# A two-layer decoder trunk on one core: four instead of three seven-product pairs in the up units, own buffers for weight halves, due times by engine

## The chip, the core and the metric

The kernel runs on one core of a Trainium2 chip. TensorE multiplies matrices into eight PSUM banks, VectorE (DVE in the profile) and ScalarE (ACT) work element by element on SBUF and PSUM, GpSimd (POOL) does little here, and SyncE (SP) issues the DMAs that bring the weights from HBM. The metric is the device time of one execution in microseconds, as a median of several runs. The time before is 2168.13 us (three runs, 2167.72 to 2169.03).

## The reference

Sequence length 256, model width 2048, two layers. Each layer has two groups of heads behind one input projection, an output projection, and an MLP with 8192 hidden columns:

```python
def hybrid_layer(x, ...):
    h = rms_norm(x, attn_norm)
    proj = h @ w_in                      # queries, keys, values, gates of both groups
    o_gla = gated linear attention (8 heads, chunks of 64), per-head rms_norm, times silu(gate)
    o_sb = stick-breaking attention (8 heads, strictly causal), per-head rms_norm
    x = x + concat(o_gla, o_sb) @ w_o    # 2048 x 2048
    hm = rms_norm(x, mlp_norm)
    up = square(relu(hm @ w_up))         # 2048 x 8192
    return x + up @ w_down               # 8192 x 2048
```

All of it is float32.

## The kernel before

**Float32 out of three matmuls.** Each operand is split into a high part, rounded to the fast float32 form of TensorE, and a low part, the rest. A product is high x high, high x low and low x high: three matmuls of 128x128 stationary by 512 moving columns. For the weights this happens on the fly: ScalarE copies the raw weights to `whi` (L1182), VectorE subtracts `raw - whi` to get `wlo` (L1186).

**Two stretches per layer.** The attention stretch (input projection, both attentions) is written in program order, with its weights split in `weight_parts` (L515). The MLP stretch begins with the last quarter of the gate projection and runs through the output projection and the MLP. It is a list of units (L1064): `g`, two `o` units, then for each of four quarters q of the hidden columns two `up` units and two `down` units (n2 = 0, 1 is the half of the columns). An `up` or `down` unit has eight pairs, a pair being 256 rows by 1024 columns of the weights (1 MB, one DMA).

**Plain and seven-product pairs.** A pair is a 2x2 by 2x2 block product: two row blocks of tokens (128 each), two blocks of the contraction, two column halves. A plain pair needs eight block products (24 matmuls) and two weight halves of 128x1024, each feeding 12 matmuls. A pair in `FAST` needs seven (21 matmuls), by Strassen's scheme in Winograd's form. For that VectorE makes three sums of raw weights (`ts` 128x1024, L1238; one 128x512 in place in `raw`, L1247; `t4` 128x512, L1243), and four things are split instead of two: row 1 of the raw pair, `t4` (half as wide), `ts`, and row 0, in this order; they feed 6, 3, 6 and 6 matmuls. The left operand needs sums too: `forms` (L391) makes four small sums on VectorE, high parts on ScalarE and low parts on VectorE. It does so for two neighbouring pairs at once if both are in the `down` list (`together`, L428). The operand of the up units is made once a layer, at the start: in `turned` (L1121), for pairs 0 to 3 behind unit o n2=0, for pairs 4 to 7 in the first two halves of the first up unit. A pair that isn't in `FAST["up"]` gets its low part by two instructions at L464. The operand of the down units is made out of each up unit's results, in `up_tail` (L1396): results are completed on VectorE (`sums_of`, `finals`), go through ReLU on ScalarE, are transposed on TensorE during the first pair of the next unit (L1427), squared, and split by `forms`.

**The planner.** The MLP stretch is scheduled by hand: each step is added to a `Plan` (L40) as a piece with an engine, an expected length, what it depends on, and a function that issues it. `run` (L68) first sets due times: TensorE's pieces are due one behind the other, without a gap; each other piece is due before the earliest of its users, less its length. Then it plays the engines forward in time: TensorE and SyncE take their pieces in list order, VectorE and ScalarE the ready piece that is due first. The order that comes out is the order of issue on each engine, and on the chip the engines follow it with semaphores.

**The ring of weight halves.** A split (`parts`, L1170) writes a pair of buffers, `whi` and `wlo`. There are five such pairs (`RING`, L1055): every fifth split uses `whi5`/`wlo5` of the pool of the MLP stretch, the others take the next one of four rotating buffers that the attention stretch uses too (`ppool`, tags `whi` and `wlo`). A split waits until TensorE has done the matmuls on the half five places before (`whi[i - RING]`, L1190). Since the four buffers rotate, splits are also tied to list order, by `last["h"]` and `last["l"]`. Raw weights have four buffers (`RAWS`), `ts` and `t4` one each.

Of the kernel before, what the change touches and what calls it, by code (L numbers as in the profile page):

```python
# [11 lines left out]
F32R = mybir.dt.float32r  # L12
# [5 lines left out]
P = 128  # L18
# [21 lines left out]
class Plan:  # L40
# [27 lines left out]
    def run(self):  # L68
        t = 0.0
        for p in self.pieces:  # L70
            if p.engine == "PE":
                p.due = t
                t += p.length
        for p in reversed(self.pieces):
            if p.engine != "PE":
                p.due = min([u.due for u in p.users], default=t) - p.length - p.lag - self.GAP
        line = {e: [p for p in self.pieces if p.engine == e] for e in ("PE", "SP")}
        free = dict.fromkeys(("PE", "SP", "DVE", "ACT"), 0.0)
        left = {p: len(p.deps) for p in self.pieces}
        at = dict.fromkeys(self.pieces, 0.0)  # L80
        ready = {"DVE": [], "ACT": []}
        order, events, count = [], [], 0
        for p in self.pieces:
            if not p.deps:
                events.append((0.0, count, p))
                count += 1
        came = set()
        while events:
            now, _, p = heapq.heappop(events)
            if p is not None:  # L90
                if p.engine in ready:
                    heapq.heappush(ready[p.engine], (p.due, count, p))
                else:
                    came.add(p)
                count += 1
            for e in free:
                if free[e] > now + 1e-9:
                    continue
                if e in ready:
                    if not ready[e]:  # L100
                        continue
                    p = heapq.heappop(ready[e])[2]
                elif line[e] and line[e][0] in came:
                    p = line[e].pop(0)
                else:
                    continue
                order.append(p)
                free[e] = now + p.length
                heapq.heappush(events, (free[e], count, None))
                count += 1  # L110
                for u in p.users:
                    at[u] = max(
                        at[u], free[e] + p.lag + (0.0 if u.engine == e else self.GAP)
                    )
                    left[u] -= 1
# [11 lines left out]
def trunk_kernel(  # L127
# [22 lines left out]
    def nm(s):  # L150
        uid[0] += 1
        return f"{s}_{uid[0]}"
# [4 lines left out]
    ppool = ctx.enter_context(tc.tile_pool(name="parts", bufs=4))  # L157
# [36 lines left out]
        return [bank_tile(b, "acc"), bank_tile(b + 1, "acc")]  # L194

    ATT = ("wg", "reset", "gmask", "mask16", "v4", "lr", "lrT", "ha", "hh", "hl", "hA", "on", "dec", "S", "kdz", "row", "bc")
    MLP = ("whi5", "wlo5", "sxh1", "sx1", "sx2", "ts", "t4", "raw2")
    MANUAL = {mybir.EngineType.PE, mybir.EngineType.DVE, mybir.EngineType.Activation}

    def tmp(tag, shape, dt=F32, bufs=2):  # L200
        pool = pools["att"] if tag in ATT else pools["mlp"] if tag in MLP else tpool
        return pool.tile(list(shape), dt, tag=tag, name=nm(tag), bufs=bufs)
# [182 lines left out]
        def both(self, k):  # L385
            return self.t[k // 2][:, k % 2].rearrange("p a t -> p (a t)")

    FAST = {"up": (1, 3, 5), "down": (2, 3, 5)}
    ORDER = {"g": (0, 1, 2, 3), "up": (0, 1, 2, 3, 4, 5, 6, 7), "down": (0, 1, 2, 3, 4, 5, 6, 7)}

    def forms(op, i, t, tag):  # L391
# [112 lines left out]
    def row_of(col):  # L504
# [7 lines left out]
        nc.vector.tensor_copy(row, pb[:, :T])  # L512
        return row

    def weight_parts(w2d, r0, c0, kt, width, fine=False, halves=1, order=lambda k: None):  # L515

        full = 2048 // kt
        raw = wpool.tile([P, kt, full], F32, tag="raw", name=nm("raw"))
        src = w2d[r0 : r0 + kt * P, c0 : c0 + width].rearrange("(k p) n -> p k n", p=P)
        step = 1 if fine else kt // halves  # L520
        for s in range(0, kt, step):
            nc.sync.dma_start(raw[:, s : s + step, :width], src[:, s : s + step, :])
        for s in range(2):
            hk = kt // 2
            hi = ppool.tile([P, hk, full], F32R, tag="whi", name=nm("whi"), bufs=4)
            lo = ppool.tile([P, hk, full], F32R, tag="wlo", name=nm("wlo"), bufs=4)
            step = 1 if fine else hk
            for q in range(0, hk, step):
                r = raw[:, s * hk + q : s * hk + q + step, :width]
                h = hi[:, q : q + step, :width]  # L530
                dep = order(s * hk + q)
                with tc.issue_after(dep) if dep else nullcontext():
                    newest["hi"] = nc.scalar.activation(h, r, AF.Copy).ins  # L533
                with tc.issue_after(st["first"]) if fine else nullcontext():
                    newest["lo"] = nc.vector.tensor_tensor(  # L535
                        lo[:, q : q + step, :width], r, f32(h), ALU.subtract
                    ).ins
            yield hi, lo
# [242 lines left out]
    for l in range(DEPTH):  # L781
# [156 lines left out]
        for b in range(2):  # L938
            t = join(unit_t(hT, wl, C_GQ + b * 256))
# [11 lines left out]
        for b in range(2):  # L951
            t = join(unit_t(hT, wl, C_GK + b * 256))
# [100 lines left out]
        add = plan.add  # L1053
        MM, TR, V2, V1, A2, A1 = 0.227, 0.108, 1.15, 0.61, 1.0, 0.55
        RING, RAWS = 5, 4  # L1055
# [20 lines left out]
        banks = {}  # L1076
        free = {}
        whi, wlo, raws = [], [], []
        up, done = {}, {}
        x_done = {}  # L1080

# [88 lines left out]
        def parts(src, readers, deps, n=2):  # L1170

            box = {}
            i = len(whi)

            def part(tag):
                if i % RING < RING - 4:
                    return tmp(tag + "5", [P, 2, 512], F32R, bufs=RING - 4)
                return ppool.tile([P, 2, 512], F32R, tag=tag, name=nm(tag), bufs=4)

            def high():  # L1180
                box["h"] = part("whi")
                nc.scalar.activation(box["h"][:, :n], src(), AF.Copy)  # L1182

            def low():
                box["l"] = part("wlo")
                nc.vector.tensor_tensor(  # L1186
                    box["l"][:, :n], src(), f32(box["h"][:, :n]), ALU.subtract
                )

            h = add("ACT", A2 if n == 2 else A1, high, deps, whi[i - RING], last.get("h"))  # L1190
            lo = add("DVE", V2 if n == 2 else V1, low, h, wlo[i - RING], last.get("l"))
            last.update(h=h, l=lo)
            whi.append([lo])
            wlo.append([])
            readers.extend((h, lo))
            return box, h, lo
# [475 lines left out]
```

## Time and profile before

| | |
|---|---|
| median of three runs | 2168.13 us |
| profiled execution: time, span | 2167.72 us, 2166.0 us |
| TensorE, VectorE, ScalarE busy | 2158.9, 1811.8, 1316.9 us |
| MLP stretch, layer 0 and 1 (first to last matmul of L1275) | 295.7 to 1087, 1372.3 to 2162 us |
| an up unit: n2=0 of a later quarter, n2=1 | 41.5, 43.3 us |
| the first up unit of a layer | 43.3 us |

Times in the profile count from the first instruction of the span. The execution takes 1.7 us more than its span, and lies 0.4 us under the median. The page groups instructions by line, engine and tiles. In a timeline a row gives start, length, engine, line, operation and tiles written and read; behind it in brackets stands the idle time of the engine before it and what ended that. A matmul's length is modelled and overlaps the next one, so pace is read from starts. VectorE's and ScalarE's instructions overlap too, by about 0.09 us, so a queue's load is less than the sum of lengths; in a table by stretches overlapping time is counted once.

### The profile page before, as it was taken

To read this page: it belongs to the slowest core of one execution; us is meant where nothing else is said; L and a number is where in the kernel's file an instruction comes from. 1 tells how busy PE (TensorE), PEld (TensorE's weight loads), DVE (VectorE), ACT (ScalarE), POOL (GpSimd) and SP (SyncE) were. 2 spreads that over 40 slices of the span, in tenths; PEclk is the share of its full clock that TensorE was granted. 3 is DMA by queue.
4 is the path that set the end of the run, shared out by engine and by line. 5 is a ranking of instruction groups with operands and counts; after the bars stand their busy time and mean duration, and the time that the engine had idled before them with its cause. 6 is when DMAs were issued, how large, how long until landed. Compare 5 with 4: busy or idle time off the path is not lost.

```text
span 2166.0 us, 27107 instructions
## 1 busy us (share of the span) xinstructions
PE 2158.9 (100%) x10352; PEld 1801.9 (83%) x10352; DVE 1811.8 (84%) x2248; ACT 1316.9 (61%) x1723; POOL 42.2 (2%) x71
## 2 busy tenths in 40 slices
PE   9999999999999999999999999999999999999999
PEld 7988888888888888888888888888888888888887
DVE  5777679998989898899857775798988999899987
ACT  5555456666566566566655554666665665665674
POOL 0020000000000000000100200000000000000000
PEclk9999999999999999999999999999999999999999
DMA  6655455565556556556546544555656655565564
GB/s 229 202 156 156 156 195 175 195 213 195 187 198 213 184 193 206 199 194 194 196 139 196 174 156 156 196 175 199 208 176 213 208 199 183 197 212 187 194 202 146
DMA packets 144358, 408.97 MB, mean 189 GB/s; under 512 B 6650, under 2 KB 31810, under 8 KB 144228
## 3 DMA queue, kind: packets, MB, share of 16 engines
q1 hardware_dynamic: 144228, 407.24, 57.0%
q8 instruction: 81, 1.33, 0.3%
q14 instruction: 49, 0.40, 0.0%
HBM read 405.12 MB, written 2.10 MB: 188 GB/s over the span
## 4 chain that ended last, share of the span: by engine, by line
PE 99%; DMA 0%; DVE 0%; SPq 0%; issue 0%; POOL 0%; ACT 0%
PE acc L552 6%; PE acc L554 6%; PE acc L553 6%; PE acc L599 3%; PE acc L603 1%; PE m__548_2787 L1275 1%; PE m__2464_11960 L1275 1%; PE m__552_2800 L1275 1%; PE m__2460_11947 L1275 1%; PE m__2561_12481 L1275 0%; PE m__2496_12142 L1275 0%; PE m__649_3321 L1275 0%; PE m__584_2982 L1275 0%; PE m__2566_12505 L1275 0%; PE m__654_3345 L1275 0%; PE m__2563_12491 L1275 0%
## 5 line engine op out<-in xcount | busy, mean ns | idle before, releaser
L1182 ACT ACTIVATE whi<-raw 128x1024 fp32r<-128x1024 f32 x592 | 617.1, 1058 | 381.4 <-PE m__2968_14364 L1275 6.9
L1186 DVE TENSOR_TENSOR wlo<-raw,whi 128x1024 fp32r<-128x1024 f32 x592 | 713.3, 1221 | 89.4 <-ACT whi L1182 83.8
L535 DVE TENSOR_TENSOR wlo<-raw,whi 128x1024 fp32r<-128x1024 f32 (+2 forms) x194 | 220.4, 1140 | 131.6 <-ACT whi L533 131.3
L533 ACT ACTIVATE whi<-raw 128x1024 fp32r<-128x1024 f32 (+2 forms) x194 | 189.8, 982 | 205.0 <-PE acc L554 156.5
L552 PE MATMUL acc<-whi,act 128*128 128x512 f32 (+2 forms) x640 | 241.7, 378 | 0.4 <-ACT act L458 0.4
L554 PE MATMUL acc<-whi,act 128*128 128x512 f32 (+2 forms) x640 | 237.0, 370 | 0.0
L553 PE MATMUL acc<-wlo,act 128*128 128x512 f32 (+2 forms) x640 | 236.2, 369 | 0.1
L1186 DVE TENSOR_TENSOR wlo<-ts,whi 128x1024 fp32r<-128x1024 f32 x104 | 127.3, 1224 | 27.4 <-ACT whi L1182 27.4
L552 PEld LDWEIGHTS acc<-whi,act 128*128 128x128 f32 x640 | 120.7, 189 | 22.5 <-issue 2.7
L554 PEld LDWEIGHTS acc<-whi,act 128*128 128x128 f32 x640 | 120.4, 188 | 20.9 <-DVE act L464 0.2
L553 PEld LDWEIGHTS acc<-wlo,act 128*128 128x128 f32 x640 | 120.7, 189 | 19.2 <-DVE wlo L535 0.6
L1058 DVE TENSOR_TENSOR ts<-raw 128x1024 f32<-128x1024 f32 x104 | 127.0, 1222 | 1.5
L1182 ACT ACTIVATE whi<-t 128x512 fp32r<-128x512 f32 x104 | 65.7, 632 | 102.6 <-DVE t L1058 90.5
L1182 ACT ACTIVATE whi<-ts 128x1024 fp32r<-128x1024 f32 x104 | 109.6, 1054 | 29.1 <-PE m__593_3021 L1275 2.1
L599 PE MATMUL acc<-act,whi 128*128 128x512 f32 x256 | 91.9, 402 | 0.0
L1186 DVE TENSOR_TENSOR wlo<-t,whi 128x512 fp32r<-128x512 f32 x104 | 71.5, 688 | 10.2 <-ACT whi L1182 10.2
L1058 DVE TENSOR_TENSOR t<-raw 128x512 f32<-128x512 f32 x104 | 71.5, 688 | 0.8
L603 PE MATMUL acc<-act,wlo 128*128 128x256 f32 x256 | 71.8, 280 | 0.0
L1058 DVE TENSOR_TENSOR raw<-ts,raw 128x512 f32<-128x512 f32 x104 | 71.3, 686 | 0.2
L599 PEld LDWEIGHTS acc<-act,whi 128*128 128x128 f32 x256 | 48.1, 188 | 11.1
L1406 ACT ACTIVATE act<-act,st 128x512 f32<-128x512 f32 x64 | 44.2, 714 | 21.3 <-DVE act L1058 21.3
L603 PEld LDWEIGHTS acc<-act,wlo 128*128 128x128 f32 x256 | 48.4, 189 | 0.1
(2130 smaller groups left out, 5007.8 us busy)
## 6 DMA issues: line engine op xcount, KB each, us to landing
raw<-in_w_up_dram SPq DMA_DIRECT2D x128, 1024.0 KB, 5.0
raw<-in_w_down_dram SPq DMA_DIRECT2D x128, 1024.0 KB, 5.2
raw<-in_w_in_dram SPq DMA_DIRECT2D x84, 1024.0 KB, 5.2
raw<-in_w_o_dram SPq DMA_DIRECT2D x32, 1024.0 KB, 5.2
raw<-in_w_in_dram SPq DMA_DIRECT2D x14, 512.0 KB, 9.3
raw<-in_w_in_dram SPq DMA_DIRECT2D x8, 544.0 KB, 3.8
out_dram<-xb SPq DMA_DIRECT2D x8, 256.0 KB, 2.7
xb<-in_x_dram SPq DMA_DIRECT2D x3, 512.0 KB, 6.9
```

What stands on the lines that cost most here:

```text
L533: newest["hi"] = nc.scalar.activation(h, r, AF.Copy).ins
L535: newest["lo"] = nc.vector.tensor_tensor(lo[:, q : q + step, :width], r, f32(h), ALU.subtract).ins
L552: nc.tensor.matmul(o, xh[:, sl], whi[:, j, :width], start=first, stop=False)
L553: nc.tensor.matmul(o, xh[:, sl], wlo[:, j, :width], start=False, stop=False)
L554: st["mm"] = nc.tensor.matmul(o, xl[:, sl], whi[:, j, :width], start=False, stop=last).ins
L599: nc.tensor.matmul(acc[f], whi[:, j, sl], op.both(k), start=(k == 0), stop=False, skip_group_check=True,)
L603: nc.tensor.matmul(acc[f][:, T:], wlo[:, j, sl], xh, start=False, stop=(k == KT - 1), skip_group_check=True,)
L1058: nc.vector.tensor_tensor(dst, a, b, op)
L1182: nc.scalar.activation(box["h"][:, :n], src(), AF.Copy)
L1186: nc.vector.tensor_tensor(box["l"][:, :n], src(), f32(box["h"][:, :n]), ALU.subtract)
L1275: nc.tensor.matmul(o, lhs, rhs, start=start and k == 0, stop=end and i + 1 == len(blocks) and k == 2, skip_group_check=onto,)
L1406: nc.scalar.activation(box[h][:, tt, :], box[h][:, tt, :], AF.Relu, scale=rr[:, tt : tt + 1],)
```

## The change

`FAST["up"]` becomes (1, 2, 4, 5) for (1, 3, 5): in each of the 16 up units four pairs instead of three go by seven products. `FAST["down"]` becomes (1, 4, 5) for (2, 3, 5), three as before. Pairs 4 and 5 now share one call of `forms` in place of 2 and 3, and `NX` keeps one more buffer for the sums of the up operand.

Each slot of the ring gets a tag with one buffer: `whi4` and `wlo4` in the MLP pool for every fifth split, and `whi0` to `whi3` and `wlo0` to `wlo3` in the pool that both stretches use, with `part_tile`. The ring stays at five. The MLP stretch picks its slots by a split's number, not by order of issue, and `part_base` carries the turn over from the attention stretch. With that the ties to list order (`last["h"]`, `last["l"]`) go.

Due times of pieces off TensorE are now set by going backward through time: of the pieces whose users are all settled, the one with the latest end comes first, and on VectorE and ScalarE it is due so that it ends before the piece of its engine that was set just before it begins. So two pieces of one engine no longer claim the same time.

```diff
@@ Plan.run
+        begins = {"DVE": t, "ACT": t}
+        unset = {p: len(p.users) for p in self.pieces if p.engine != "PE"}
+        last = []
+
+        def settled(p):
+            for d in p.deps:
+                if d in unset:
+                    unset[d] -= 1
+                    if not unset[d]:
+                        push(d)
+
+        def push(p):
+            end = min([u.due for u in p.users], default=t) - p.lag - self.GAP
+            heapq.heappush(last, (-end, -at_of[p], p))
...
         for p in reversed(self.pieces):
-            if p.engine != "PE":
-                p.due = min([u.due for u in p.users], default=t) - p.length - p.lag - self.GAP
+            if p.engine == "PE":
+                settled(p)
+        while last:
+            end, _, p = heapq.heappop(last)
+            p.due = min(-end, begins.get(p.engine, t)) - p.length
+            if p.engine in begins:
+                begins[p.engine] = p.due
+            settled(p)
@@
-    FAST = {"up": (1, 3, 5), "down": (2, 3, 5)}
+    FAST = {"up": (1, 2, 4, 5), "down": (1, 4, 5)}
@@
+    part_turn = [0]
+
+    def part_tile(tag, turn, shape):
+        slot = f"{tag}{turn % 4}"
+        return ppool.tile(shape, F32R, tag=slot, name=nm(tag), bufs=1)
+
@@ weight_parts
-            hi = ppool.tile([P, hk, full], F32R, tag="whi", name=nm("whi"), bufs=4)
-            lo = ppool.tile([P, hk, full], F32R, tag="wlo", name=nm("wlo"), bufs=4)
+            hi = part_tile("whi", part_turn[0], [P, hk, full])
+            lo = part_tile("wlo", part_turn[0], [P, hk, full])
+            part_turn[0] += 1
@@ parts
                 if i % RING < RING - 4:
-                    return tmp(tag + "5", [P, 2, 512], F32R, bufs=RING - 4)
-                return ppool.tile([P, 2, 512], F32R, tag=tag, name=nm(tag), bufs=4)
+                    return tmp(f"{tag}{4 + i % RING}", [P, 2, 512], F32R, bufs=1)
+                return part_tile(tag, i % RING - (RING - 4) + part_base, [P, 2, 512])
...
-            h = add("ACT", A2 if n == 2 else A1, high, deps, whi[i - RING], last.get("h"))
-            lo = add("DVE", V2 if n == 2 else V1, low, h, wlo[i - RING], last.get("l"))
-            last.update(h=h, l=lo)
+            h = add("ACT", A2 if n == 2 else A1, high, deps, whi[i - RING])
+            lo = add("DVE", V2 if n == 2 else V1, low, h, wlo[i - RING])
```

More of the change, by code (lines that the diff above doesn't have):

```diff
@@ L73, in run @@
                 t += p.length
-        for p in reversed(self.pieces):
-            if p.engine != "PE":
-                p.due = min([u.due for u in p.users], default=t) - p.length - p.lag - self.GAP
+        begins = {"DVE": t, "ACT": t}
[10 more added lines that the diff above has]
+            heapq.heappush(last, (-end, -at_of[p], p))
+        at_of = {p: i for i, p in enumerate(self.pieces)}
+        for p in self.pieces:
+            if p in unset and not p.users:
+                push(p)
+        for p in reversed(self.pieces):
+            if p.engine == "PE":
[6 more added lines that the diff above has]
+            settled(p)
         line = {e: [p for p in self.pieces if p.engine == e] for e in ("PE", "SP")}
@@ L196, in trunk_kernel @@
     ATT = ("wg", "reset", "gmask", "mask16", "v4", "lr", "lrT", "ha", "hh", "hl", "hA", "on", "dec", "S", "kdz", "row", "bc")
-    MLP = ("whi5", "wlo5", "sxh1", "sx1", "sx2", "ts", "t4", "raw2")
+    MLP = (*(f"{t}{i}" for t in ("whi", "wlo") for i in range(4, 12)), "sxh1", "sx1", "sx2", "ts", "t4", "raw2")
     MANUAL = {mybir.EngineType.PE, mybir.EngineType.DVE, mybir.EngineType.Activation}
@@ L1078, in trunk_kernel @@
         whi, wlo, raws = [], [], []
+        part_base = part_turn[0] % 4
         up, done = {}, {}
```

## The prediction

> **What bounds the kernel now.** I read the page first (engines, then the chain that ended last), then busy time by stretch, then the timelines of TensorE and VectorE in the two-matmul-per-weight part of the layer.
>
> ```profile
> span 2166.0 us, 27107 instructions
> ...
> PE 2158.9 (100%) x10352; PEld 1801.9 (83%) x10352; DVE 1811.8 (84%) x2248; ACT 1316.9 (61%) x1723; POOL 42.2 (2%) x71
> ...
> PE 99%; DMA 0%; DVE 0%; SPq 0%; issue 0%; POOL 0%; ACT 0%
> ```
>
> TensorE is the chain. But a busy matmul row can hide a wait, so its pace must be read from starts. Here is the first matmul of the fourth product of a seven-product pair, and the first one of the pair after it:
>
> ```profile
> 458.00 0.39 PE L1275 MATMUL m__841_4203<-whi,act 128*128 128x512 f32 x1
> ...
> 460.71 0.39 PE L1275 MATMUL m__816_4102<-whi,act 128*128 128x512 f32 x1
> ```
>
> Twelve matmuls start in 460.71 - 458.00 = 2.71 us, 0.226 us each: back to back, no wait. A product (three matmuls) is 0.68 us. So time falls one for one with matmuls removed, as long as the weight halves keep arriving. Who delivers them, and with how much room? One round of units (down n2=1, up n2=0, up n2=1, down n2=0), then the first up unit of a layer:
>
> ```profile
> core 0: us, PE busy (x) PEld busy (x) DVE busy (x) ACT busy (x) POOL busy (x), PEclk, DMA share, GB/s
> 535.29:576.77 41.48, 41.48 (x185) 34.35 (x183) 36.75 (x40) 22.11 (x24) 0.00 (x0) 1.00 0.60 198
> 576.77:618.25 41.48, 41.48 (x185) 34.35 (x183) 36.44 (x39) 23.50 (x26) 0.00 (x0) 1.00 0.61 202
> 618.25:661.55 43.30, 43.30 (x200) 36.01 (x199) 40.09 (x47) 30.39 (x38) 0.00 (x0) 1.00 0.60 200
> 661.55:704.83 43.28, 43.28 (x200) 36.00 (x199) 39.90 (x48) 30.45 (x41) 0.00 (x0) 1.00 0.59 194
> sum 169.54, PE 169.54 PEld 140.70 DVE 153.18 ACT 106.45 POOL 0.00; mean PE 42.38 PEld 35.17 DVE 38.29 ACT 26.61 POOL 0.00
> ...
> 405.42:448.71 43.29, 43.29 (x200) 36.00 (x199) 40.87 (x56) 28.41 (x42) 0.00 (x0) 1.00 0.57 194
> ```
>
> VectorE is the next bound: 153.18 of 169.54 us, so 16.4 us free in a round, and only 2.4 us in the first up unit. ScalarE has 63 us free and the DMA engines 40%. Part of VectorE's free time is not lack of work: it is ahead, and the ring of five weight halves is full. Two rows of an up unit show that:
>
> ```profile
> 601.18 1.23 DVE L1186 TENSOR_TENSOR wlo<-raw,whi 128x1024 fp32r<-128x1024 f32 x1 [1.44 <-ACT whi L1182]
> ...
> 602.81 1.06 ACT L1182 ACTIVATE whi<-raw 128x1024 fp32r<-128x1024 f32 x1 [1.66 <-PE m__1056_5204 L1275]
> ```
>
> VectorE waits for ScalarE, and ScalarE for TensorE to release a slot.
>
> **The change, part by part.** *Removed:* in each of 16 up units one pair more goes by seven products instead of eight: 16 x 3 x 0.226 = 10.9 us of TensorE. The down units keep three such pairs at other places (1, 4, 5 for 2, 3, 5): nothing on TensorE.
>
> *Added,* by these groups (the last column but one has the mean ns of one):
>
> ```profile
> L1182 ACT ACTIVATE whi<-raw 128x1024 fp32r<-128x1024 f32 x592 | 617.1, 1058 | 381.4 <-PE m__2968_14364 L1275 6.9
> L1186 DVE TENSOR_TENSOR wlo<-raw,whi 128x1024 fp32r<-128x1024 f32 x592 | 713.3, 1221 | 89.4 <-ACT whi L1182 83.8
> ...
> L1182 ACT ACTIVATE whi<-t 128x512 fp32r<-128x512 f32 x104 | 65.7, 632 | 102.6 <-DVE t L1058 90.5
> ```
>
> A plain pair costs VectorE two wide subtractions. A seven-product pair costs three wide and one narrow, and three sums (ts wide, raw and t narrow): two wide and three narrow more. What one costs the queue is the spacing of starts, not the duration:
>
> ```profile
> 637.50 1.22 DVE L1186 TENSOR_TENSOR wlo<-raw,whi 128x1024 fp32r<-128x1024 f32 x1
> 638.64 0.69 DVE L1058 TENSOR_TENSOR raw<-ts,raw 128x512 f32<-128x512 f32 x1
> 639.24 1.22 DVE L1186 TENSOR_TENSOR wlo<-raw,whi 128x1024 fp32r<-128x1024 f32 x1
> ```
>
> 1.14 us wide, 0.60 us narrow: 2 x 1.14 + 3 x 0.60 = 4.1 us more a pair, 66 us in all. ScalarE gets one wide and one narrow copy more, under 1.7 us, in 63 us of free time: no cost.
>
> The Trainium skill says otherwise about the spacing: "VectorE: DVE Perf Modes", section "The DRAIN you can't avoid", has the next operation start only when the pipeline is empty. By that a pair would cost 4.5 us, some 2 us would come on top at each tight place below, and the forecast would be about 2166. The trace does not agree (1.14 us between starts of 1.22 us operations), and the same page grants an earlier start to an operation that is not held; the sum goes by the starts.
>
> *VectorE after.* Two up units in a round: 153.2 + 8.2 = 161.4 us against 169.5 - 1.4 = 168.2 us. On the whole it fits, 96% full. Whether it fits in time is decided at the last wide subtraction of pair 5: from pair 1 on four of five pairs are now short ones, and TensorE eats such a pair in 21 x 0.226 = 4.75 us where VectorE needs 3 x 1.14 + 0.60 + 2.34 = 6.4 us.
>
> *An up unit with n2=0.* Here VectorE is through with the last unit's results and splits the narrow sum of pair 1:
>
> ```profile
> 577.92 0.69 DVE L1186 TENSOR_TENSOR wlo<-t,whi 128x512 fp32r<-128x512 f32 x1 [0.18 <-ACT whi L1182]
> ...
> 606.01 0.39 PE L1275 MATMUL m__1067_5245<-whi,act 128*128 128x512 f32 x1
> ```
>
> The last half of pair 5 was wanted at 606.01, and will be at 605.3. From 577.9 that leaves 27.4 us. Work: rest of pair 1 (0.6 + 1.14 + 1.14), pairs 2, 4, 5 (19.2), pair 3 (2.3): 24.4 us. About 3 us to spare, less some tenths of waits for ScalarE, so no stall.
>
> *An up unit with n2=1* has 1.8 us of transposes on TensorE more (43.30 against 41.48) and the forms of the down operand on VectorE. These are wanted a unit later, and due times can put them off; with pair 4 and 5 the wide form moves into the down unit, where pairs 2 and 3 leave room. No stall.
>
> *The first up unit of a layer* has no such work to put off: the forms of its own operand are wanted by its own pairs.
>
> ```profile
> 406.58 0.69 DVE L1186 TENSOR_TENSOR wlo<-t,whi 128x512 fp32r<-128x512 f32 x1 [0.18 <-ACT whi L1182]
> 412.68 0.29 DVE L405 TENSOR_TENSOR e<-t 128x128 f32<-128x128 f32 x1
> 413.94 0.87 DVE L464 SCALAR_TENSOR_TENSOR act<-m__752_3789,gcol_b,act 128x256 fp32r<-128x256 f32 x2
> 418.38 0.55 DVE L424 TENSOR_TENSOR sxh<-e,sxh 128x384 fp32r<-128x384 f32 x1
> 419.45 1.22 DVE L1186 TENSOR_TENSOR wlo<-raw,whi 128x1024 fp32r<-128x1024 f32 x1
> ...
> 436.48 0.39 PE L1275 MATMUL m__765_3844<-whi,act 128*128 128x512 f32 x1
> ```
>
> The first row is the narrow split of pair 1, the last one the use of the last half of pair 5, which comes 0.7 us earlier after. From 406.6 to 435.8 there are 29.2 us, and the work is the 24.4 us from above, forms of pairs 4 and 5 (each 1.26 for the four sums, 412.68 to 413.94, and 1.07 for the two subtractions, 418.38 to 419.45: 4.7 us together), of pairs 6 and 7 (1.6, twice 413.94 to 414.73), and up to 0.8 of norm steps that may go later: 30.7 to 31.5 us. It is late by 1.5 to 2.3 us; I take 2 us, in both layers: 4 us. TensorE takes its work in list order, so all of it stands behind that half. Bounds for each: 0, if the new order finds all of it elsewhere, and 4, if ScalarE's queue adds as much again.
>
> *Order and buffers.* Own buffers and due times add no instruction. Splits out of list order only lose two waits. The price of a bad order is unseen: from below 0; from above about 0.5 us in each of the other 14 up units, the size of the short waits for ScalarE (0.18 to 0.5 us) in front of VectorE rows. I take 0. Loads keep their number and size on SP's queue, and share 0.60 leaves them time.
>
> **Sum.** Profiled execution 2167.72 us (span 2166.0 and 1.7 around it) - 10.9 + 4.0 = 2160.8; the median of the runs is 0.4 higher, so **2161.2 us**.
>
> **Rivals.** *No stall at all:* the planner moves the forms into the gaps. For it: 3 us of room in plain units. Against: 2.4 us free in the first up unit. 2168.1 - 10.9 = 2157.2. Nothing can go lower, since TensorE has no wait left to lose.
>
> *Small stalls in every up unit:* 14 x 0.5 = 7 and 4 in the first ones: 2168.1. For it: four short pairs of five with a ring of five halves; against: down units with pairs 2 and 3 side by side run without a stall.
>
> *Slower: VectorE becomes the bound,* because its free time comes where the ring is full and can't be filled. Up units then grow by what does not fit. If half of the free time counts: n2=1 (3.2 free) 4.1 + 0.7 - 1.6 = 3.2 us, eight times; n2=0 (5.0 free) 2.3 us, six times; the first ones (2.4 free, 1.6 forms more) 5.2 us, twice: 50 us against 10.9, some 2207. At all of the free time it is 8 x 1.6 + 2 x 4.0 = 21 us without help of the neighbours, 2178. So it decides whether the forms, 4 us, really move into the down unit: with that, n2=1 has none left. Against it: those forms have a full unit's time.
>
> *TensorE loses its pace after a stall.* In its first microseconds eight transposes take 1.97 us, later 1.03:
>
> ```profile
> 4.62 1.97 PE L448 MATMUL ps<-ident,xb 128*128 128x128 f32 x8 [0.88 <-DMA xb<-in_x_dram]
> ...
> 12.00 1.03 PE L448 MATMUL ps<-ident,xb 128*128 128x128 f32 x8
> ```
>
> The slow pace lasted some 3.3 us (4.6 to 7.9, 14 transposes); at half pace that loses 1.6 us. If both stalls were as long as that, 2157.2 + 2 x (3.3 + 1.6) = 2167. This is the rule of the Trainium skill, "TensorE: Matmul & The Clock Gate", section "What's actually happening": an idle window of about 3.4 us brings the slow clock. The granted clock reads 1.00 in all rows above, so the trace neither shows nor excludes it.
>
> **How the numbers follow.** Forecast 0.42, no stall 0.26, small stalls everywhere 0.17, VectorE bound 0.12, lost pace 0.03. The likeliest is 2161.2. The range runs from 2156.6 (no stall, 0.6 for the runs' scatter) to 2171 (small stalls and the upper bound of the first units), leaving out most of the VectorE case. A measurement of this kernel tells about 0.2%, 4.3 us, from no change: faster means under 2163.8. Of the forecast's 0.42, 0.04 lies above that: faster 0.64; same 0.04 + 0.16 + 0.03 + 0.01 = 0.24; slower 0.12.
>
> **What would show it.** Right: 48 matmuls fewer, VectorE 66 us busier at most, TensorE starts 0.226 us apart in plain up units, and one gap of about 2 us near pair 4 or 5 of the first up unit of each layer, ended by VectorE. Wrong: gaps in front of every pair 5 or of unit starts, a chain that runs over VectorE, or forms of the down operand that TensorE waits for.

## The result, and the profile after

The changed kernel takes 2162.71 us (median of nine runs, 2161.46 to 2163.32) against 2168.93 us of the kernel before on the same chip (nine runs, 2167.47 to 2169.52): ratio 0.9972, 95% interval 0.9962 to 0.9982. It is 6.2 us faster, where 6.9 were forecast (2168.1 to 2161.2). (The kernel before is 0.8 us slower here than in the three runs that the forecast started from.)

The page of the changed kernel, engines and chain of work:

```profile
span 2161.0 us, 27114 instructions
...
PE 2150.1 (99%) x10304; PEld 1793.6 (83%) x10304; DVE 1871.0 (87%) x2336; ACT 1339.9 (62%) x1759; POOL 40.5 (2%) x71
...
PE 97%; DVE 2%; ACT 0%; DMA 0%; issue 0%; SPq 0%; POOL 0%; DVEq 0%
```

TensorE has its 48 matmuls fewer (10352 to 10304). VectorE has 88 instructions and 59 us more. In the chain VectorE has gained 2%: somewhere TensorE now waits for it. Where, the stretches of the units show (first and second up unit of layer 0; then the round that the prediction showed: down n2=1, up n2=0, up n2=1, down n2=0). The columns are the length, then busy time and instructions of each engine, and the granted clock:

```profile
core 0: us, PE busy (x) PEld busy (x) DVE busy (x) ACT busy (x) POOL busy (x), PEclk, DMA share, GB/s
406.62:451.58 44.96, 43.20 (x197) 35.29 (x196) 44.09 (x62) 30.39 (x45) 0.00 (x0) 1.00 0.53 184
451.58:494.18 42.60, 42.60 (x197) 35.44 (x196) 42.21 (x51) 31.23 (x40) 0.00 (x0) 1.00 0.62 211
...
537.48:578.96 41.48, 41.48 (x185) 34.35 (x183) 36.60 (x39) 22.43 (x24) 0.00 (x0) 1.00 0.57 197
578.96:619.76 40.80, 40.80 (x182) 33.78 (x180) 40.04 (x44) 24.88 (x28) 0.00 (x0) 1.00 0.59 207
619.76:662.38 42.62, 42.62 (x197) 35.45 (x196) 41.96 (x51) 31.64 (x42) 0.00 (x0) 1.00 0.57 194
662.38:705.66 43.28, 43.28 (x200) 36.00 (x199) 42.08 (x50) 29.41 (x39) 0.00 (x0) 1.00 0.59 204
sum 168.18, PE 168.18 PEld 139.58 DVE 160.68 ACT 108.36 POOL 0.00; mean PE 42.05 PEld 34.89 DVE 40.17 ACT 27.09 POOL 0.00
```

The round went from 169.54 to 168.18 us, that is 2 x 0.68: both its up units fell by their three matmuls, and nothing else moved. VectorE's 160.68 us fit into it, though 42 of 42.6 us in an n2=1 unit leave almost nothing. The first up unit is the exception: 44.96 us where 42.6 would be left of 43.29, so 2.36 us lost. The other layer's first unit loses the same. So the account is 10.9 - 2 x 2.36 = 6.2 us.

The loss lies in two places, seen in TensorE's timeline (start, length, and in brackets the idle time before the row and what ended it):

```profile
430.19 0.39 PE L1307 MATMUL m__738_3732<-whi,act 128*128 128x512 f32 x1
431.49 0.50 PE L1307 MATMUL m__738_3732<-wlo,act 128*128 128x512 f32 x1 [0.91 <-DVE wlo L1219]
...
434.79 0.39 PE L1307 MATMUL m__736_3722<-whi,act 128*128 128x512 f32 x1
436.03 0.50 PE L1307 MATMUL m__736_3722<-wlo,act 128*128 128x512 f32 x1 [0.85 <-DVE wlo L1219]
```

From 430.19 to 431.49 are 1.30 us where matmuls start 0.23 apart, and from 434.79 to 436.03 1.24: gaps of 1.07 and 1.01 us. The remaining 0.3 us of the loss are starts behind a gap that come a little later than 0.23 us. In both cases the high half was there, and TensorE waits for the low half, the work of VectorE. VectorE's timeline at these places:

```profile
417.60 1.23 DVE L1219 TENSOR_TENSOR wlo<-ts,whi 128x1024 fp32r<-128x1024 f32 x1 [0.46 <-ACT whi L1215]
...
430.75 0.68 DVE L1219 TENSOR_TENSOR wlo<-t,whi 128x512 fp32r<-128x512 f32 x1
...
434.77 1.21 DVE L1219 TENSOR_TENSOR wlo<-raw,whi 128x1024 fp32r<-128x1024 f32 x1
```

The row at 430.75 is the narrow split of pair 4, the one at 434.77 the first split of pair 5; TensorE goes on as they end. From 417.60, where VectorE last waited for another engine, to 436 it is hardly ever idle:

```profile
406.62:417.60 10.98, 10.98 (x58) 9.27 (x57) 10.28 (x18) 9.54 (x21) 0.00 (x0) 1.00 0.49 181
417.60:436.00 18.40, 16.67 (x73) 13.15 (x71) 18.30 (x25) 12.68 (x15) 0.00 (x0) 1.00 0.43 137
```

In the second row VectorE is busy 18.30 of 18.40 us, TensorE 16.67: a plain queue that is too long for its stretch.

**A warning on two single executions.** The two profiled ones differ by 5.0 us (2167.72 to 2162.71), not by 6.2, and the 1.2 are at the very start. The changed kernel's first matmuls, then those of the kernel before:

```profile
10.62 0.63 PE L585 MATMUL acc<-wlo,act 128*128 128x512 f32 x1
11.04 0.63 PE L586 MATMUL acc<-whi,act 128*128 128x512 f32 x1
```

```profile
9.74 0.39 PE L553 MATMUL acc<-wlo,act 128*128 128x512 f32 x1
9.97 0.40 PE L554 MATMUL acc<-whi,act 128*128 128x512 f32 x1
```

They start 0.42 apart here and 0.23 there. The MLP stretch of layer 0 then begins at 296.90 against 295.69 us. In the profiled executions of the other kernels below it begins anywhere between 295.3 and 297.3, so this belongs to the execution and not to the kernel. From there on each MLP stretch is 3.1 us shorter (791.7 to 788.6) and the attention stretch between them is unchanged.

### The profile page after: what moved, and what is told of

Read it like the earlier page. It is cut to its first block, busy times and chain, and to the rows that moved or that the text cites. A ratio compares the mean times of both kernels' runs of the same rounds, so it can differ in the third digit from the quotient of the medians.

```text
span 2161.0 us, 27114 instructions
## 1 busy us (share of the span) xinstructions
PE 2150.1 (99%) x10304; PEld 1793.6 (83%) x10304; DVE 1871.0 (87%) x2336; ACT 1339.9 (62%) x1759; POOL 40.5 (2%) x71
## 4 chain that ended last, share of the span: by engine, by line
PE 97%; DVE 2%; ACT 0%; DMA 0%; issue 0%; SPq 0%; POOL 0%; DVEq 0%
PE acc L584 6%; PE acc L586 6%; PE acc L585 6%; PE acc L631 3%; PE acc L635 1%; DVE wlo L1219 1%; PE m__2515_12049 L1307 1%; PE m__552_2800 L1307 1%; PE m__2511_12036 L1307 1%; PE m__548_2787 L1307 1%; PE m__2547_12231 L1307 0%; PE m__584_2982 L1307 0%; PE m__2611_12568 L1307 0%; PE m__648_3319 L1307 0%; PE m__2617_12593 L1307 0%; PE m__654_3344 L1307 0%
## 5 line engine op out<-in xcount | busy, mean ns | idle before, releaser
L1215 ACT ACTIVATE whi<-ts 128x1024 fp32r<-128x1024 f32 x120 | 126.9, 1058 | 95.8 <-PE m__999_4899 L1307 6.5
L1219 DVE TENSOR_TENSOR wlo<-ts,whi 128x1024 fp32r<-128x1024 f32 x120 | 146.6, 1221 | 40.3 <-ACT whi L1215 39.9
L1090 DVE TENSOR_TENSOR ts<-raw 128x1024 f32<-128x1024 f32 x120 | 146.2, 1218 | 0.7
L1215 ACT ACTIVATE whi<-t 128x512 fp32r<-128x512 f32 x120 | 75.0, 625 | 35.2 <-DVE t L1090 7.5
L1219 DVE TENSOR_TENSOR wlo<-t,whi 128x512 fp32r<-128x512 f32 x120 | 82.1, 684 | 8.9 <-ACT whi L1215 8.9
L1090 DVE TENSOR_TENSOR t<-raw 128x512 f32<-128x512 f32 x120 | 82.1, 684 | 1.0
L1090 DVE TENSOR_TENSOR raw<-ts,raw 128x512 f32<-128x512 f32 x120 | 81.9, 682 | 0.2
```

Source lines behind the costliest of these rows:

```text
L1090: nc.vector.tensor_tensor(dst, a, b, op)
L1219: nc.vector.tensor_tensor(box["l"][:, :n], src(), f32(box["h"][:, :n]), ALU.subtract)
```

## The experiments

Twelve kernels, each timed against the kernel before. Beside the median stands what the MLP units lost in the profiled execution: the sum over all units of the length beyond that of the same unit before, less 0.68 us for each pair that became a short one. With 10.9 us removed (21.8 where the down units get a fourth pair too, 0 for the old pairs), 10.9 minus the loss should be the gain, and the last two columns hold the two side by side.

| kernel | median us | ratio to before, 95% interval | lost in units, us | gain by units / measured, us |
|---|---|---|---|---|
| as changed | 2162.71 | 0.9972 (0.9962 to 0.9982) | 4.7 | 6.2 / 6.2 |
| order_alone | 2168.78 | 0.9999 (0.9990 to 1.0008) | 0.0 | 0.0 / 0.3 |
| pairs_alone | 2178.68 | 1.0048 (1.0031 to 1.0065) | 20.9 | -10.0 / -9.6 |
| own_and_pairs | 2174.22 | 1.0025 (1.0015 to 1.0035) | 16.2 | -5.3 / -5.2 |
| due_and_pairs | 2204.68 | 1.0165 (1.0150 to 1.0180) | 45.5 | -34.6 / -35.6 |
| tie_scalar | 2198.35 | 1.0137 (1.0121 to 1.0154) | 39.2 | -28.3 / -29.4 |
| one_sum | 2160.49 | 0.9962 (0.9949 to 0.9975) | 2.7 | 8.2 / 8.5 |
| first_6_early | 2161.01 | 0.9962 (0.9948 to 0.9975) | 2.6 | 8.3 / 8.3 |
| first_apart | 2160.91 | 0.9961 (0.9948 to 0.9973) | 2.7 | 8.2 / 8.4 |
| down_old | 2163.36 | 0.9974 (0.9963 to 0.9984) | 5.2 | 5.7 / 5.9 |
| up_0235 | 2167.97 | 0.9995 (0.9986 to 1.0005) | 9.5 | 1.4 / 1.1 |
| up_1235 | 2178.03 | 1.0042 (1.0027 to 1.0057) | 19.7 | -8.8 / -9.0 |
| down_1245 | 2226.64 | 1.0269 (1.0252 to 1.0286) | 77.4 | -55.6 / -57.6 |

The two agree within 0.5 us in all but the three slowest kernels (within 2.0 there). So the time of every one of these kernels is the matmuls it removes less what its MLP units lose, and the unit in which it loses is told by its profile.

### The pairs alone, and the planner alone

**order_alone** keeps new due times, own buffers and no ties, with the old pairs; **pairs_alone** is the kernel before with the new pairs.

```diff
order_alone, against the changed kernel
-    FAST = {"up": (1, 2, 4, 5), "down": (1, 4, 5)}
+    FAST = {"up": (1, 3, 5), "down": (2, 3, 5)}
pairs_alone, against the kernel before
-    FAST = {"up": (1, 3, 5), "down": (2, 3, 5)}
+    FAST = {"up": (1, 2, 4, 5), "down": (1, 4, 5)}
```

> The changed planner and buffers with the old pairs (up 1, 3, 5; down 2, 3, 5). Theory (the gain is 48 matmuls, TensorE had no wait to lose): the time of before, 2168 to 2169.5 us, and no TensorE gap over 0.4 us in the MLP stretch. Rival (order and buffers bring time of their own): 2166 or less.

> The new pairs (up 1, 2, 4, 5; down 1, 4, 5) with the old planner, rotating buffers and list order. Theory (VectorE fits only because the forms of the down operand can be put off): besides the first up unit of each layer the up units with n2=1 stall too, by 1 to 2 us each, eight of them: 2168 to 2176. Rival (VectorE's load alone decides, order does nothing): the changed kernel's 2162.7 with the same two stalls a layer of 1 us each.

The planner alone is worth nothing: no unit changes its length by 0.1 us, and there was no wait of TensorE left for it to remove. The pairs alone make the kernel slower, by 10 us. The first up units lose 3.94 us each, the second ones 2.33, the six other n2=1 units 1.3 to 1.6, the n2=0 and the down units nothing. That is more than was expected of it (2168 to 2176), in the kind of place that was expected. TensorE in an n2=1 unit of pairs_alone:

```profile
639.65 0.50 PE L1275 MATMUL m__1137_5533<-wlo,act 128*128 128x512 f32 x1 [0.41 <-DVE wlo L1186]
```

And VectorE just before it (of L424 a part of the rows, then the split that TensorE waits for):

```profile
632.09 0.69 DVE L424 TENSOR_TENSOR act<-act,act 128x512 fp32r<-128x512 f32 x1
...
633.77 0.68 DVE L424 TENSOR_TENSOR act<-act,act 128x512 fp32r<-128x512 f32 x1
...
635.50 0.68 DVE L424 TENSOR_TENSOR act<-act,act 128x512 fp32r<-128x512 f32 x1
...
638.38 1.22 DVE L1186 TENSOR_TENSOR wlo<-raw,whi 128x1024 fp32r<-128x1024 f32 x1
```

L424 is in `forms`: low parts of the down operand, which no one needs before the next unit, stand ahead of a weight split that TensorE needs at once. All four 128x512 rows of this kind lie within this unit; in the changed kernel (L449) two do, and the other two have moved into the down unit behind it, where six stand. This is the putting off that the prediction counted on, 1.2 us of it. It fits the old due times, which gave every piece its own latest end, as if it had the engine to itself; with four short pairs too many claim the same microseconds.

### Which half of the planner change carries it

The next two take one half each: **due_and_pairs** has new due times with the rotating buffers and ties of before, **own_and_pairs** own buffers, no ties, and the old due times.

```diff
due_and_pairs, against the kernel before: the new block in Plan.run, and
-    FAST = {"up": (1, 3, 5), "down": (2, 3, 5)}
+    FAST = {"up": (1, 2, 4, 5), "down": (1, 4, 5)}
own_and_pairs, against the changed kernel: in Plan.run the block of begins, unset, settled and push goes, and
+            if p.engine != "PE":
+                p.due = min([u.due for u in p.users], default=t) - p.length - p.lag - self.GAP
```

> New pairs and new due times; buffers rotate and splits keep list order as before. Theory: due times are what puts the forms off, list order costs little since a split can hardly come before its forerunner: within 1.5 us of the changed kernel, 2161.5 to 2164. Rival (the ties cost): stalls in every up unit, over 2166.

> New pairs and own buffers without ties to list order; due times as before. Theory (due times carry it): near to the pairs alone, 2167 to 2176. Rival (free order carries it): within 1.5 us of the changed kernel's 2162.7.

own_and_pairs came as the theory had it: the second up units lose 1.95 us each, the six other n2=1 units 1.1, as in pairs_alone but somewhat less. due_and_pairs is a clear miss: the ties were thought to cost next to nothing, and the kernel is 42 us slower than the changed one. The first up units lose 4.4 us, the second ones and those of the second and third quarters with n2=1 lose 3.2 to 3.9, also units `o` n2=1 (2.8), and four down units 1.7 to 1.8. ScalarE and TensorE at the end of such an up unit:

```profile
672.59 0.63 ACT L1207 ACTIVATE whi<-t 128x512 fp32r<-128x512 f32 x1 [4.47 <-DVE t L1083]
673.12 1.04 ACT L1207 ACTIVATE whi<-ts 128x1024 fp32r<-128x1024 f32 x1
674.07 0.58 ACT L1322 ACTIVATE m__1227_5916<-xb 128x512 f32<-128x512 f32 x1
```

```profile
674.70 0.50 PE L1300 MATMUL m__1227_5916<-whi,act 128*128 128x512 f32 x1 [2.25 <-ACT m__1227_5916 L1322]
```

L1322 (L1329 in the changed kernel, L1330 in tie_scalar below) writes the residual into the PSUM bank on which the down unit begins; this is the bank's seed. It needs 0.58 us. But it stands in ScalarE's queue behind two copies, and the first of them waits 4.47 us for VectorE's sum `t`. That is not the whole of it. The bank is free only when VectorE has read the up unit's result out of it, and VectorE does that late here:

```profile
672.39 0.68 DVE L1083 TENSOR_TENSOR act<-m__1139_5535,t 128x512 f32<-128x512 f32 x1
```

This row ends at 673.07. The seed starts 1.0 us later, at 674.07: about 1.0 of the 2.25 us is the queue of ScalarE, the rest this late row and the seed itself. In the changed kernel the same row starts at 658.80, 3.6 us before the down unit begins (662.38). ScalarE reads there:

```profile
660.14 0.58 ACT L1329 ACTIVATE m__1222_5899<-xb 128x512 f32<-128x512 f32 x1
...
661.35 0.59 ACT L1329 ACTIVATE m__1224_5911<-xb 128x512 f32<-128x512 f32 x1
661.87 0.62 ACT L1215 ACTIVATE whi<-t 128x512 fp32r<-128x512 f32 x1
```

There two of the unit's four seeds come before the narrow copy, which has no wait. To see whether the tie on ScalarE alone does the harm, **tie_scalar** adds only that one to the changed kernel:

```diff
-            h = add("ACT", A2 if n == 2 else A1, high, deps, whi[i - RING])
+            h = add("ACT", A2 if n == 2 else A1, high, deps, whi[i - RING], last.get("h"))
+            last["h"] = h
```

> The changed kernel, own buffers and new due times, with ScalarE's splits alone tied to list order again. Theory (with both ties the long gaps, 2.4 us at the start of down units, came from ScalarE: seeds of the banks stood behind the split of the narrow sum): most of that kernel's 38 us of gaps come back, over 20 us, 2180 us or more. Rival (VectorE's tie or the rotating buffers did it): gaps of 4 to 10 us in all, 2162 to 2169.

As the theory had it, it brings back 35.6 of the 42 us (2198.35 against 2162.71, each timed beside the kernel before). ScalarE in tie_scalar shows the same picture, the narrow copy with its wait, and the seed of the bank behind it:

```profile
673.22 0.63 ACT L1215 ACTIVATE whi<-t 128x512 fp32r<-128x512 f32 x1 [4.58 <-DVE t L1090]
...
674.70 0.58 ACT L1330 ACTIVATE m__1227_5916<-xb 128x512 f32<-128x512 f32 x1
```

Here too VectorE reads the bank out late, until 673.70, and the seed starts 1.0 us after that. The waits of TensorE in unit `o` n2=1 and the first up unit of that kernel (what waits, for what, us in total, times, longest) show the seeds late in a second place, and one wait of another kind:

```profile
PE m__734_3717 L1308 <- DVE act L449: 3.7, 1, 3.7
PE m__663_3375 L1308 <- ACT m__663_3375 L1330: 0.8, 1, 0.8
```

The first row is in the first up unit, which loses 5.5 us here: the operand's forms are late. ScalarE had their high parts done at 418.3, but VectorE takes the low part at 434.11, behind splits (424.96 in the changed kernel), so here it is VectorE's order that comes out badly and not a wait of ScalarE. Over the whole kernel TensorE's waits for seeds add up to 14 us and those for forms to 7.5, and four of the six longest waits cost clock besides (last section). So the tie is shown to cost 35.6 us; that a waiting copy holds up a seed is shown for 1.0 us at a time, and why VectorE's rows come late under the tie stays open. In sum the halves need each other. New due times under ties lose 45.5 us, free order under old due times 16.2, both old 20.9, both new 4.7.

### Is the stall in the first up unit a matter of VectorE's load?

**one_sum** leaves out three of the four small sums that VectorE makes in the forms of the up operand:

```diff
@@ sums
+            if tag == "sxh":
+                nc.vector.tensor_tensor(e[:, :, 0, :], a21, a11, ALU.subtract)
+                box["e"] = e[:, :, 0:1, :].to_broadcast([P, w, 3, P])
+                return
```

> The changed kernel with one instead of four VectorE sums in the forms of the up operand (three of its four sums are left out, high and low parts stay). Theory (the two stalls of 1 us in each layer's first up unit are VectorE's load, and the forms of pairs 4 and 5 make it too much): 1.9 us of VectorE work less in that unit takes the gaps there from 2.1 to at most 0.4 us, 2158.5 to 2160 us in all. Rival (the stalls come from where the planner puts its pieces, or from ScalarE): the gaps stay over 1.5 us a layer, 2162 to 2163.

The result lies between the two: of two gaps one is left, in both layers. TensorE and VectorE of one_sum:

```profile
434.84 0.50 PE L1311 MATMUL m__736_3716<-wlo,act 128*128 128x512 f32 x1 [0.85 <-DVE wlo L1223]
```

```profile
429.35 0.29 DVE L431 TENSOR_TENSOR e<-t 128x128 f32<-128x128 f32 x1
429.55 0.69 DVE L1223 TENSOR_TENSOR wlo<-t,whi 128x512 fp32r<-128x512 f32 x1
...
433.56 1.22 DVE L1223 TENSOR_TENSOR wlo<-raw,whi 128x1024 fp32r<-128x1024 f32 x1
```

In the changed kernel these two splits stand at 430.75 and 434.77, 1.20 and 1.21 us later; 0.2 of that is the unit's own later start (406.62 against 406.41), so 1.0 us is gained. That is what one set of sums can give: three quarters of its 1.26 us are 0.95. So load it is: work taken out ahead of a split brings it forward one for one, and of two gaps of together 2.1 us the first 1.0 is covered. But it is one set only, that of pair 5 at 429.4. The sums of pair 4 lie at 413, ahead of VectorE's last wait (417.60), and what is saved before a wait is waited away: in one_sum VectorE has a new wait of 0.87 us at 414.05. The expectation had counted both.

The other way to the same is to move pairs. **first_6_early** and **first_apart** change the order of pairs in the first up unit of a layer, so that a plain pair stands between short ones:

```diff
@@ pair_order, at its head
+                if units[u] == ("up", 0, 0):
+                    return (0, 1, 2, 3, 6, 4, 5, 7), set(FAST["up"])   # first_6_early
+                    return (0, 1, 3, 2, 6, 4, 5, 7), set(FAST["up"])   # first_apart
```

> The changed kernel, with pair 6 ahead of pair 4 in the first up unit of each layer alone (0, 1, 2, 3, 6, 4, 5, 7). Theory (VectorE is late there by 2 us at the end of a run of short pairs): a plain pair in front of pairs 4 and 5 gives VectorE 5.4 - 2.3 = 3.2 us before they are wanted, both gaps go, 2158 to 2159.5 us. Rival (the unit as a whole is too full, the lateness only moves behind pair 5 or into the next unit): gaps of 1.5 to 2 us a layer elsewhere, 2162 to 2163.

> The same with pairs 1 and 2 taken apart as well in the first up unit (0, 1, 3, 2, 6, 4, 5, 7). Theory: nothing more to gain than with pair 6 early, 2158 to 2159.5 us. Rival (the unit is too full): 2162 to 2163.

Both gaps are gone in both kernels, and 1.0 of the 2.36 us comes back in each layer (a loss of 4.7 us falls to 2.6 or 2.7); where pair 2 stands makes no difference. So both results, 2161.0 and 2160.9 us, lie between theory and rival: the rest has moved behind the unit. TensorE at the start of the second up unit of first_apart, and VectorE just before:

```profile
450.19 0.47 PE L1309 MATMUL m__824_4114<-whi,act 128*128 128x512 f32 x1 [0.95 <-DVE act L1090]
```

```profile
449.37 0.68 DVE L1090 TENSOR_TENSOR act<-m__735_3720,t 128x512 f32<-128x512 f32 x1
```

VectorE is late with the unit's last results, and until it has read them out the PSUM bank isn't free. VectorE still ends about a microsecond too late; it is only noticed elsewhere. These are the fastest complete versions here, by about 2.1 us below the changed kernel when each is set against the kernel before; their intervals overlap with its own, and the two weren't timed side by side with it.

### Does it matter which pairs are short?

**down_old** keeps the new up pairs and takes the old down pairs; **up_1235** and **up_0235** place four short pairs elsewhere; **down_1245** gives the down units four as well.

```diff
-    FAST = {"up": (1, 2, 4, 5), "down": (1, 4, 5)}
+    FAST = {"up": (1, 2, 4, 5), "down": (2, 3, 5)}      # down_old
+    FAST = {"up": (1, 2, 3, 5), "down": (1, 4, 5)}      # up_1235
+    FAST = {"up": (0, 2, 3, 5), "down": (1, 4, 5)}      # up_0235
+    FAST = {"up": (1, 2, 4, 5), "down": (1, 2, 4, 5)}   # down_1245
```

> The changed kernel with the down pairs of before (2, 3, 5). Theory (the shift to 1, 4, 5 moves the wide form out of the up unit with n2=1, but forms can be put off anyway): VectorE has 0.9 us more in those eight units, in which it is almost full, so gaps of 0 to 1 us each: 2162.5 to 2170. Rival (the place of the down pairs does not matter): within 1 us of the changed kernel.

> Up pairs 1, 2, 3, 5: only pair 5 needs sums in the first up unit, those of pairs 1, 2, 3 are made in the unit before. Theory: the first up unit has 1.6 us less to do, its gaps shrink to some 0.5 us; three short pairs side by side cost VectorE 5 us against TensorE, more than the 3 us of room, so that small gaps of 0.5 to 1 us come up in the other 14 up units: 2165 to 2172. Rival (room enough): 2158 to 2160.

> Up pairs 0, 2, 3, 5: only pair 5 needs sums in the first up unit, and no more than two short pairs stand side by side. Theory: the gaps in the first up unit shrink to 0.5 us or less and none come up elsewhere: 2157.5 to 2160, faster than the changed kernel. Rival (pair 0 is short just when the last unit's results are due on VectorE): gaps at the unit starts, over 2163.

> Four short pairs in the down units too (1, 2, 4, 5): 48 matmuls, 10.9 us of TensorE less again, 66 us more on VectorE. Theory (VectorE is full): a round of four units asks 164.8 us of VectorE against 166.8 of TensorE, and 86.5 against 85.2 in the two heavy units, so each of eight rounds stalls by 2 to 5 us: 2168 to 2192. Rival (the new order finds the room): 2152 to 2157.

The place of the down pairs is worth nothing that can be measured: down_old loses 5.2 us in its units where the changed kernel loses 4.7. The place of the up pairs is worth up to 15 us. up_1235 missed its range on the slow side (2178.0, 2165 to 2172 expected): the first up units lose 1.7 us instead of some 0.5, and the loss in the others isn't spread evenly. With the same three short pairs in a row each later n2=1 unit loses 1.75 us, each later n2=0 unit only 0.2, so the forms of the down operand have a part in it. TensorE in an n2=1 unit:

```profile
640.69 0.51 PE L1307 MATMUL m__1141_5547<-wlo,act 128*128 128x512 f32 x1 [0.80 <-DVE wlo L1219]
```

In up_0235, whose pair 0 is a short one, the second up units lose 1.1 us, the other n2=1 units 0.8, and the first only 1.2, all of it at the start of the units. In the n2=1 units the transposed results are squared and split there (in the first up unit TensorE waits for low parts of its own operand, L489). TensorE in an n2=1 unit and the ScalarE row it waits for:

```profile
625.37 0.50 PE L1307 MATMUL m__1159_5603<-whi,act 128*128 128x512 f32 x1 [0.20 <-ACT act L1467]
```

```profile
624.72 0.59 ACT L1467 ACTIVATE act<-m__1149_5571 128x512 f32<-128x512 f32 x1
```

The theory had put this kernel level with the changed one; the rival, that pair 0 would run into the unit's start, was right. down_1245 has 48 matmuls fewer again, and takes 64 us more time than the changed kernel. Its direction was foreseen, its size was not (2168 to 2192 expected): down n2=0 units lose 2.6 us in the median (1.5 to 4.1), n2=1 up units 3.7 (1.8 to 5.4), the first up units 4.7 and 6.3, the two units `o` n2=1 6.9 and 6.5. TensorE in its first up unit waits 3.2 us in one place:

```profile
440.74 0.50 PE L1307 MATMUL m__734_3717<-whi,act 128*128 128x512 f32 x1 [3.20 <-DVE act L449]
```

Here it is the operand's forms that are late. Elsewhere in this kernel TensorE waits for seeds (up to 4.3 us), splits (up to 1.8) and squares (up to 1.5), so several kinds of step are late.

## Why the prediction was right

**Matmuls, -10.9 us: right.** 41.48 to 40.80 in plain up units is the 3 x 0.226 us.

**The stall of the first up unit, +4.0: right in unit and cause, a little small.** 4.7 us. The gaps are 2.08 us in each layer, within the 1.5 to 2.3 of lateness that was worked out, and 0.3 us come on top by slower starts behind them, which the sum had left out. That is the whole difference between 6.9 and 6.2 us. Three steps on the way were not right. The stall was to stand in one piece before the last half of pair 5; it came in two, at pair 4's narrow split and pair 5's first one. The count ran as if VectorE had no wait behind its start; it still waits 0.46 us at 417.60, and one_sum shows that work ahead of this wait is free. And the count began in the wrong place: it took the narrow split of pair 1 to stand 1.2 us behind the unit's start as before (406.58 against 405.42), but in the changed kernel it stands 1.4 us ahead of it:

```profile
405.18 0.68 DVE L1219 TENSOR_TENSOR wlo<-t,whi 128x512 fp32r<-128x512 f32 x1
405.78 0.68 DVE L1090 TENSOR_TENSOR xb<-m__654_3344,act 128x512 f32<-128x512 f32 x1
```

Of the 2.6 us that this gives, 1.2 go to two results of unit `o` that are now read out behind it (405.78 and 407.51) and some 0.5 to waits. So the place and the kind of the stall were worked out, and that its size came so close is in part luck.

**No stall in the n2=0 units: right,** in this and in all kernels with these pairs, also those with the old planner: the later n2=0 up units lose 0.0 us in each. That fits the count of 24.4 us in 27.4, though VectorE has little left there over the whole unit (40.04 us busy of 40.80).

**No stall in the n2=1 units: right, and this is the step that decided the sign.** The prediction said that "due times can put them off", the forms of the down operand. Without the new due times they are not put off: pairs_alone and own_and_pairs lose 13 and 11 us in those units. So the prediction was right where it gave the planner that job, but it named due times alone and set no price on the other case. Under the ties the same due times lose 22 us in those units (due_and_pairs).

**"Order and buffers ... I take 0": right for the changed kernel, and for the wrong reason in one point.** Alone they are worth nothing (order_alone). With the new pairs they are worth 16 us (2178.7 to 2162.7). "Splits out of list order only lose two waits" named the size of the edit and not its price: the tie of ScalarE's splits alone costs 35.6 us under the new due times. The times of due_and_pairs and tie_scalar, 2204.7 and 2198.4, lie where the rival "VectorE becomes the bound" was put (2178 to 2207). Load alone does not explain them: VectorE has the same 2336 instructions in them as in the changed kernel. What differs is the order (in due_and_pairs the buffers too).

**VectorE's cost: right by starts.** 59 us more busy time against "66 us at most"; 7.5 us in the round where 8.2 were worked out. By the rule of the Trainium skill weighed there ("VectorE: DVE Perf Modes", section "The DRAIN you can't avoid"), the first units would by the prediction's estimate have lost some 4 us more; the measured time speaks for the spacing of starts.

**Lost pace after a stall: it did not happen here** (the granted clock reads 1.00 in the first up units of both layers, whose gaps last about 1 us), but see the last section.

**The range:** its upper end was added up 1 us short. Small stalls (7 us) and 4 us in each first unit on top of 2157.2 make 2172, not 2171. The measured 2162.7 lies far from either.

## What to carry to other kernels

When matmuls are traded for work on another engine, count that engine's queue from its last wait to the deadline, in spacing of starts, for each kind of unit; the average over the kernel (87% busy here) hides the one unit in which it doesn't fit. In a queue that runs in order, ask of every instruction that may wait what stands behind it: a 0.6 us copy with a late input held a bank's seed back by 1.0 us at a time, and the tie that put it there cost 36 us in all. And test the parts of a joint change together as well as alone: the planner was worth nothing with the old pairs, the pairs cost 10 us with the old planner, and together they gained 6.

## What the runs showed of the hardware

The clock can fall after a wait of little more than 2 us. In due_and_pairs TensorE waits 2.2 to 2.3 us at the start of six down units. After the one that ends at 674.70, its matmuls:

```profile
676.50 0.63 PE L1300 MATMUL m__1227_5916<-whi,act 128*128 128x512 f32 x1
676.93 0.63 PE L1300 MATMUL m__1228_5919<-whi,act 128*128 128x512 f32 x1
677.35 0.63 PE L1300 MATMUL m__1228_5919<-wlo,act 128*128 128x512 f32 x1
```

They start 0.43 us apart and not 0.23. The stretches behind this wait and behind another one, of the same length, that ends at 502.9 (the last columns but two are the granted clock):

```profile
675.00:679.00 4.00, 4.00 (x12) 3.10 (x11) 3.43 (x4) 3.08 (x6) 0.00 (x0) 0.57 0.01 4
679.00:690.00 11.00, 11.00 (x58) 9.27 (x57) 8.57 (x13) 9.57 (x15) 0.00 (x0) 1.00 0.40 109
...
503.00:507.00 4.00, 4.00 (x22) 3.39 (x23) 3.66 (x5) 4.00 (x7) 0.00 (x0) 1.00 0.02 4
```

The clock is 0.57 for about 4 us and then whole again; behind the other wait it stays at 1.00. Four of the six waits lost it (0.57 to 0.68 in the 4 us behind them), each at some 1.6 us more (the four down units lose 1.7 to 1.8 us, the other two 0.15).

Waits of other lengths stand in other kernels. In down_1245 TensorE waits 18 times for 1.3 to 1.9 us, and behind none of these waits do matmuls start 0.43 us apart. The 4 us behind the longest, of 1.86 us:

```profile
1962.90:1966.90 4.00, 4.00 (x22) 3.41 (x23) 3.84 (x5) 4.00 (x7) 0.00 (x0) 1.00 0.00 0
```

Of the four waits of 2.4 us in tie_scalar two lost the clock, of the two of 3.2 us in down_1245 one, and all five of 3.7 to 4.3 us in these two kernels did (0.50 to 0.68). Between 1.9 and 2.2 us no trace here has a wait. The Trainium skill ("TensorE: Matmul & The Clock Gate", section "What's actually happening") says that a free-running window of activity decides, of about 3.4 us. That a wait of one length loses the clock in some places and not in others agrees with a window that runs freely; that 2.25 us of idleness suffice is less than a whole window of it, and here the measurement decides.
